# Moving the transposes of a hybrid decoder trunk into longer bursts: both heads of a differential pair in one step, all blocks of rotated queries and keys in one step

## The chip, the core and the metric

The kernel runs on one NeuronCore of a Trainium2 chip. The metric is the device time of one execution in microseconds, as the median of several runs. Beside the runs there is one execution recorded by the hardware profiler, from which all rows below come. Its engines are called PE (TensorE matmuls; its weight loads are PEld), DVE (VectorE), ACT (ScalarE), POOL (GpSimd) and SP (SyncE, which issues the DMAs).

## The reference, cut to what matters

Two layers over a sequence of 256 tokens and 1024 features. Each layer has a mixer of three head groups and a cross attention to a memory of 256 rows; a last RMSNorm follows.

```python
def hybrid_mixer(hn, ...):
    proj = hn @ w_in
    (mq, mk, mv, mg, dq_, dk_, dv_, dg, sq, sk, sv, sg) = jnp.split(proj, cuts, axis=-1)
    a_o = moba_attention(rope(mq), rope(mk), mv)             # 6 heads of 64; here plain causal softmax
    b_o = diff_attention(rope(dq_), rope(dk_), dv_, lam, ...)  # 4 heads, two softmaxes each
    c_o = stick_breaking_attention(sq, sk, sv)               # 6 heads of 64
    merged = concat([a_o * silu(mg), b_o * silu(dg), c_o * silu(sg)])
    return merged @ w_out

def diff_attention(q, k, v, lam, head_norm_g, lam_init):
    p = softmax(causal(q @ k.T * scale))          # sub-heads 2h and 2h+1
    a = p[:, :, 0] - lam * p[:, :, 1]
    o = rms_norm(a @ v, head_norm_g)
    return o * (1.0 - lam_init)

for l in range(2):
    h = h + hybrid_mixer(rms_norm(h), ...)
    h = h + memory_cross_attention(rms_norm(h), rms_norm(mem), ...)
return rms_norm(h)
```

## The kernel before, in words

Every large product is done three times in a reduced fp32 form: the weight tile that a DMA brings (`wraw`) is split by ACT into a rounded part `whi` (line 156) and by DVE into the rest `wlo` (line 157), the activations likewise into `xh` and `xl`, and PE multiplies `whi` with `xh`, `wlo` with `xh` and `whi` with `xl`. `load_next` issues the load and the two splits of one weight tile, five tiles ahead of its use, into six buffers: a split waits until PE has done with the tile that lay in its buffer.

**Order on PE.** PE's instructions stand in the order in which the Python code emits them. The projections are loops (`w_stationary`, lines 409 to 442; `t_stationary`, lines 444 to 459; `mixed`) which call `tick` after each 12 products of 256 columns or 6 of 512. The attention work is written as generators, called jobs: each `yield pe, wait` says how much PE time the step has just taken, in the code's own clock `self.now`, and how long to wait until the next step is due. `tick` (line 115) adds the products' time to the clock and runs the steps that have come due, between two groups of products. So the constants at the top of the file (`COMBINE_NEXT`, `PT_WAIT` and so on) decide behind which group of products a step stands.

**Order on ACT and DVE.** Each of the two engines works through one list. That list is not in the order of emission: the framework's scheduler chooses it from its own estimate of when each operand is ready. A row of the built program tells it; the source doesn't.

**The steps around the change**, in one mixer:

- `transposed` (line 760) transposes the rotated queries and keys by PE against the identity (line 765), four 128x128 blocks into one PSUM bank, and ACT copies the bank (line 767). It runs for the differential heads (`tj`, two banks, copied to `dT`) beside the projection `T3`, and for the MoBA heads (`tj2` with two banks and `tj3` with one, copied to `mT`) beside the memory keys' projection `K`.
- `diff(c)` for c = 0 and 1 handles two differential heads: scores, softmax numerators, a combination of the two softmaxes on DVE (lines 784 to 790), then the transposes of the two results (`p_transposed`, line 591: three transposes and one ACT copy each). The job with c = 1 then multiplies all four heads with their values (`pv`, line 602), squares the outputs, sums the squares on PE (`row_sums`, line 353), takes the inverse root of the sums on DVE and ACT (`inv_root_rows`, lines 360 to 369: the scaled sums are called `dms`, the root `dy`, a temporary `dt`) and scales the gates 3 and 4 with it (line 820).
- `memory_k` (line 503) runs the projection `K`, whose outputs DVE scales into `xq` (line 510) and splits into `xkT` and `xkl`.
- `moba(c)` (line 836) takes scores, numerators (`numerators`, line 575: DVE masks and takes the maximum at line 581, ACT exponentiates at line 586), the scaling (line 847), transposes and `pv`.
- The output projection `out_part` (line 869) takes its eight inputs in the order of `OUT_ORDER`: first the three stick-breaking chunks, then chunks 3 and 4, the differential ones, then the MoBA ones. `more` (line 872) splits each chunk's gate into `xh` on ACT (line 169) and `xl` on DVE (line 170). The inputs from chunks 3 and 4 are `xh3`, `xl3`, `xh4`, `xl4`.

Of the kernel before, what the change touches and what calls it, by code (L numbers as in the profile page):

```python
# [59 lines left out]
DIFF_WAIT, DIFF_PACE, COMBINE_WAIT, COMBINE_NEXT = 6500, 8500, 3750, 1700  # L60
MOBA_WAIT, MOBA_PACE, MOBA_NEXT = 5200, 2000, 1100
X_WAIT, PT_WAIT, ROPE_WAIT = 6000, 950, 8800
# [5 lines left out]
MEM_WAIT, MEM_NORM, X_RSTD = 6000, 28000, 1600  # L68
MOBA_START, SB_START, DIFF_START = 14350, 1500, 1000
PT_LAST = 1300  # L70
MIX_NORM = 14000
ROWS_WAIT, DROWS_WAIT = 11000, 3600
HALVED = 5
# [4 lines left out]
class Trunk:  # L78
# [588 lines left out]
    def mixer(self, l):  # L667
# [15 lines left out]
        def norm():  # L683
            if l == 0:
                squares()
                yield 0, SQ_WAIT
            yield from self.rstd(sq, nr, wait=RSTD_WAIT[l])
            self.tables("silu_and_others")
            yield 0, max(0.0, t2 - self.now)
            gates("W2", o2)  # L690

        njob = self.job(norm(), MIX_NORM if l else FIRST_NORM)
        t2 = self.now + 10500
# [41 lines left out]
        def together(pending, last, first, then):  # L735

            pending.append((first, then))
            if last:
                outs = [f() for f, _ in pending]
                for o, (_, f) in zip(outs, pending):  # L740
                    f(o)
# [16 lines left out]
        jobs = [self.job(sb(c, i > 0), SB_START + SB_PACE * i) for i, c in enumerate((1, 2, 0))]  # L758

        def transposed(x, blocks, dst):  # L760
            for j in range(0, len(blocks), 2):
                ps = self.bank()
                for b in range(2):
                    for t in range(2):
                        nc.tensor.transpose(ps[:, b * 256 + t * 128:b * 256 + t * 128 + 128],  # L765
                                            x[:, t, blocks[j + b] * 128:blocks[j + b] * 128 + 128], self.ident)
                nc.scalar.activation(dst[j // 2], ps, AF.Copy)
                yield 440, 0

        t0 = token("T0", "tq")  # L770
        self.rope(t0, 16, 32, 4, 8)
        dT = [A([128, 512], f"dT{i}") for i in range(2)]
        tj = self.job(transposed(t0, [0, 1, 2, 3], dT), ROPE_WAIT)

        def diff(c):

            self.finish(tj)
            qk = []
            for s in range(4 * c, 4 * c + 4):
                cb, r = s // 4, 32 * (s % 4)  # L780
                qk.append([x[r:r + 32, cb * 256:cb * 256 + 256] for x in dT])
            pr = [self.numerators(ps, 32 ** -0.5) for ps in self.score_quad(qk)]
            yield 1100, DIFF_WAIT
            for j in range(2):
                (p1, r1), (p2, r2) = pr[2 * j:2 * j + 2]
                nc.vector.tensor_scalar(r2, r2, self.lam[:, l:l + 1], None, OP.mult)
                for t, cc in ((0, slice(0, 128)), (1, slice(128, 384))):
                    nc.vector.tensor_scalar(p2[:, cc], p2[:, cc], r2[:, t:t + 1], None, OP.mult)
                    nc.vector.scalar_tensor_tensor(p1[:, cc], p1[:, cc], r1[:, t:t + 1], p2[:, cc],
                                                   OP.mult, OP.subtract)  # L790
            yield 0, COMBINE_WAIT
            pts = []
            for j in range(2):
                pts.append(self.p_transposed(pr[2 * j][0]))
                yield 330, (PT_WAIT if j else COMBINE_NEXT)
            sq = []

            def gated(o):
                q2 = self.work.tile([128, 256], F32, name="sq")
                nc.scalar.activation(q2, o, AF.Square)  # L800
                g = self.gate[3 + len(sq)]
                nc.vector.scalar_tensor_tensor(g, o, self.hg[:, l:l + 1], g, OP.mult, OP.mult)
                sq.append(q2)

            dp.append((pts, c))
            if c == 0:
                return
            outs = [self.pv(lambda j, t: tok["t2"][:, t, 256 + 64 * (2 * c + j):320 + 64 * (2 * c + j)], pts)
                    for pts, c in dp]
            hi, lo = [self.act.tile([128, 512], R, name=n, tag=g) for n, g in (("dnh", "dT0"), ("dnl", "dT1"))]  # L810
            for i, o in enumerate(outs):
                gated(o)
                self.split(sq[i], hi[:, i * 256:i * 256 + 256], lo[:, i * 256:i * 256 + 256])
            yield 1440, DROWS_WAIT
            ps = self.row_sums(self.halfm, hi, lo, 512)
            ms, y, t = [self.work.tile([128, 512], F32, name=n, tag="prob", bufs=5) for n in ("dms", "dy", "dt")]
            self.inv_root_rows(ps, -1.0 / 64, y, t, ms)
            for i in range(2):
                g = self.gate[3 + i]
                nc.vector.tensor_tensor(g, y[:, i * 256:i * 256 + 256], g, OP.mult)  # L820
            yield 480, 0

        tok["t3"] = token("T3", "t3")

        dj = [self.job(diff(c), DIFF_START + DIFF_PACE * c) for c in range(2)]
        t2 = tok["t2"] = token("T2", "t2")
        self.rope(t2[:, :, 0:256], 4, 64, 8, 0)
        t1 = token("T1", "tq")
        self.rope(t1, 8, 64, 8, 0)

        mT = [A([128, 512], f"mT{i}") for i in range(3)]
        tj2 = self.job(transposed(t1, [0, 1, 2, 3], mT[0:2]), ROPE_WAIT)
        tj3 = self.job(transposed(t2, [0, 1], mT[2:3]), ROPE_WAIT)
        blk = lambda i: mT[i // 2][:, (i % 2) * 256:(i % 2) * 256 + 256]

        def moba(c):
# [14 lines left out]
            for j in range(2):  # L851
                pts.append(self.p_transposed(ps[j]))
                yield 330, (PT_LAST if j else MOBA_NEXT)
            together(mp, c > 0, lambda: self.pv(lambda j, t: tok["t3"][:, t, 64 * (2 * c + j):64 * (2 * c + j) + 64],
# [282 lines left out]
```

## Time and profile before

| | before |
|---|---|
| median of 3 runs | 400.91 us (400.55 to 401.03) |
| the profiled execution | 399.81 us, of which its span is 398.1 us |
| PE busy | 390.6 us (98% of the span) |
| DVE busy, ACT busy | 320.8 us (81%), 282.4 us (71%) |
| granted TensorE clock, mean | 0.999 |
| DMA | 64.10 MB, mean 161 GB/s |

The span runs from the first to the last instruction; the profiled execution's own time is 1.71 us longer. Busy time of PE counts overlapping, pipelined matmuls once, and their ends are modelled, so what a matmul costs PE is read from the distance between two starts, not from its duration.

### The profile page before, as it was taken

How to read it: one execution, taken by the hardware profiler on the slowest of the kernel's cores; microseconds unless marked ns; L12 is line 12 of the kernel's file. 1: busy time of each engine (PE TensorE's matmuls, PEld its weight loads, DVE VectorE, ACT ScalarE, POOL GpSimd, SP SyncE). 2: the span in 40 equal slices, each digit the busy share in tenths (PEclk: the TensorE clock that was granted, in tenths of full speed). 3: DMA queues.
4: the chain of work that ended last, by engine and by line, in shares of the span. 5: the costliest groups of instructions: out<-in, count | busy, mean ns of one | idle time of the engine just before them, and what ended most of it. 6: DMA issues, size and time to landing. Idle time of an engine off the chain costs nothing.

```text
span 398.1 us, 7706 instructions
## 1 busy us (share of the span) xinstructions
PE 390.6 (98%) x2803; PEld 355.2 (89%) x2803; DVE 320.8 (81%) x784; ACT 282.4 (71%) x593; POOL 43.7 (11%) x109
## 2 busy tenths in 40 slices
PE   8999999999999999999999999999999999999993
PEld 8999988777899989988999999888788999998983
DVE  5988868788969869889797864876997896797964
ACT  7889588776866868559486934879687667675843
POOL 5688950000000000000000000000000000000000
PEclk9999999999999999999999999999999999999999
DMA  8995794334353343721747765443346433361002
GB/s 287 351 321 173 244 314 151 132 108 138 131 186 130 107 156 109 239 80 53 265 121 267 242 210 169 160 158 105 94 154 225 132 120 127 108 212 53 1 2 105
DMA packets 19190, 64.10 MB, mean 161 GB/s; under 512 B 2384, under 2 KB 2768, under 8 KB 19152
## 3 DMA queue, kind: packets, MB, share of 16 engines
q1 hardware_dynamic: 19152, 63.61, 47.2%
q8 instruction: 22, 0.36, 0.4%
q14 instruction: 16, 0.13, 0.1%
HBM read 62.55 MB, written 1.05 MB: 160 GB/s over the span
## 4 chain that ended last, share of the span: by engine, by line
PE 89%; DVE 6%; ACT 3%; issue 1%; ACTq 0%; DVEq 0%
PE bank L428 39%; PE bank L455 8%; PE bank L457 7%; PE bank L456 7%; PE bank L1013 3%; PE bank L607 2%; PE bank L596 2%; DVE wlo L157 2%; PE bank L948 1%; PE bank L659 1%; ACT whi L156 1%; PE bank L765 1%; PE bank L483 1%; PE bank L482 1%; PE bank L481 1%
## 5 line engine op out<-in xcount | busy, mean ns | idle before, releaser
L157 DVE TENSOR_TENSOR wlo<-wraw,whi 128x1024 fp32r<-128x1024 f32 (+2 forms) x118 | 137.3, 1169 | 33.8 <-ACT whi L156 32.3
L156 ACT ACTIVATE whi<-wraw 128x1024 fp32r<-128x1024 f32 (+2 forms) x118 | 118.2, 1011 | 40.0 <-PE bank L428 19.5
L428 PE MATMUL bank<-xh,whi 128*128 128x256 f32 x416 | 119.1, 287 | 0.0
L428 PE MATMUL bank<-xh,wlo 128*128 128x256 f32 x416 | 117.3, 283 | 0.0
L428 PE MATMUL bank<-xl,whi 128*128 128x256 f32 x416 | 117.1, 283 | 0.0
L428 PEld LDWEIGHTS bank<-xh,whi 128*128 128x128 f32 x416 | 79.4, 191 | 1.4 <-issue 0.7
L428 PEld LDWEIGHTS bank<-xh,wlo 128*128 128x128 f32 x416 | 79.5, 192 | 0.2 <-DVE wlo L157 0.2
L428 PEld LDWEIGHTS bank<-xl,whi 128*128 128x128 f32 x416 | 79.5, 192 | 0.0
L455 PE MATMUL bank<-whi,xh 128*128 128x512 f32 x128 | 52.0, 407 | 0.0
L456 PE MATMUL bank<-wlo,xh 128*128 128x512 f32 x128 | 50.1, 392 | 0.0
L457 PE MATMUL bank<-whi,xl 128*128 128x512 f32 x128 | 50.1, 391 | 0.0
L586 ACT ACTIVATE prob<-prob,mx 128x128 f32<-128x128 f32 (+1 forms) x56 | 24.8, 445 | 10.9 <-DVE mx L583 10.9
L455 PEld LDWEIGHTS bank<-whi,xh 128*128 128x128 f32 x128 | 24.1, 188 | 6.2 <-issue 2.0
L457 PEld LDWEIGHTS bank<-whi,xl 128*128 128x128 f32 x128 | 24.0, 188 | 5.3
L456 PEld LDWEIGHTS bank<-wlo,xh 128*128 128x128 f32 x128 | 24.1, 188 | 4.1
L314 ACT ACTIVATE xh<-h 128x256 fp32r<-128x256 f32 x32 | 14.5, 497 | 6.6 <-DVE h L310 6.3
L428 PE MATMUL bank<-mh,whi 128*128 128x256 f32 x64 | 18.8, 294 | 0.0
L581 DVE CUSTOM_DVE_ANT_0 prob<-bank,cmask 128x128 f32<-128x128 f32 (+1 forms) x56 | 17.9, 350 | 0.3
L428 PE MATMUL bank<-ml,whi 128*128 128x256 f32 x64 | 18.1, 282 | 0.0
L428 PE MATMUL bank<-mh,wlo 128*128 128x256 f32 x64 | 18.1, 282 | 0.0
L325 ACT ACTIVATE sq<-h 128x256 f32<-128x256 f32 x28 | 11.4, 410 | 6.4 <-DVE sqacc L326 5.9
L647 DVE SCALAR_TENSOR_TENSOR sbr<-sbe,sbr 128x384 f32<-128x384 f32 x12 | 6.4, 556 | 11.7 <-ACT sbr L646 11.7
(285 smaller groups left out, 790.2 us busy)
## 6 DMA issues: line engine op xcount, KB each, us to landing
wraw<-in_w_dram SPq DMA_DIRECT2D x107, 512.0 KB, 3.8
wraw<-in_w_dram SPq DMA_DIRECT2D x10, 256.0 KB, 4.4
wraw<-in_memT_dram SPq DMA_DIRECT2D x4, 512.0 KB, 4.6
h<-in_xT_dram SPq DMA_DIRECT2D x3, 256.0 KB, 4.5
out_dram<-wraw SPq DMA_DIRECT2D x2, 288.0 KB, 2.2
wraw<-in_gfin_dram SPq DMA_DIRECT2D x1, 512.0 KB, 4.9
out_dram<-wraw SPq DMA_DIRECT2D x2, 224.0 KB, 2.2
h<-in_xT_dram SPq DMA_DIRECT2D x1, 280.0 KB, 3.0
```

What stands on the lines that cost most here:

```text
L156: nc.scalar.activation(hi[:, c], raw[:, c], AF.Copy)
L157: nc.vector.tensor_tensor(lo[:, c], raw[:, c], hi[:, c].bitcast(F32), OP.subtract)
L314: nc.scalar.activation(h, src[k], AF.Copy, scale=g)
L325: nc.scalar.activation(s, src[k], AF.Square)
L428: nc.tensor.matmul(outs[m], st[:, kk, c], x[k], start=k + p == 0 and m % 2 == 0, stop=k == n - 1 and p == 2, skip_group_check=True)
L455: nc.tensor.matmul(outs[t], xh[k][:, c], whi[:, kk, :], start=first, stop=False)
L456: nc.tensor.matmul(outs[t], xh[k][:, c], wlo[:, kk, :], start=False, stop=False)
L457: nc.tensor.matmul(outs[t], xl[k][:, c], whi[:, kk, :], start=False, stop=last)
L581: nc.vector.tensor_tensor_reduce(s[:, c], ps[:, c], self.cmask[:, c], 1.0, -3.0e38, OP.add, OP.max, accum_out=m[:, t:t + 1])
L586: nc.scalar.activation(s[:, c], s[:, c], AF.Exp, bias=m[:, t:t + 1], scale=scale, accum_out=sm[:, t:t + 1])
L596: nc.tensor.transpose(ps[:, b * 128:b * 128 + 128], p[:, b * 128:b * 128 + 128], self.ident)
L1013: nc.tensor.matmul(out[:, 0:w], x[:, r], w_, start=m == 0 and not seeded, stop=m == 11, skip_group_check=True)
```

## The change

Two generators yield less often. `transposed` now emits all its banks in one step and reports their PE time together. `diff` waits `COMBINE_NEXT` first and then emits the transposes of both heads of its pair in one step, followed by a wait of the new constant `DIFF_PT` (1400) in place of `PT_WAIT` (950). The line numbers of the changed file are one larger from line 71 on and one or two larger behind `transposed`.

```diff
@@ -68,6 +68,7 @@
 PT_LAST = 1300
+DIFF_PT = 1400
 MIX_NORM = 14000
@@ -758,6 +759,7 @@
         def transposed(x, blocks, dst):
+
             for j in range(0, len(blocks), 2):
                 ps = self.bank()
                 for b in range(2):
@@ -765,7 +767,7 @@
                 nc.scalar.activation(dst[j // 2], ps, AF.Copy)
-                yield 440, 0
+            yield 220 * len(blocks), 0
@@ -789,10 +791,9 @@
             yield 0, COMBINE_WAIT
-            pts = []
-            for j in range(2):
-                pts.append(self.p_transposed(pr[2 * j][0]))
-                yield 330, (PT_WAIT if j else COMBINE_NEXT)
+            yield 0, COMBINE_NEXT
+            pts = [self.p_transposed(pr[2 * j][0]) for j in range(2)]
+            yield 660, DIFF_PT
             sq = []
```

No instruction is added or removed on any engine, and the list of DMAs is the same. On PE, per layer, four pairs of bursts become one: 4 and 4 transposes beside `T3`; 3 and 3 beside `T1` (for c = 0); 3 and 3 at the end of `T1` (for c = 1); and beside `K` a burst of 8 and, 12 products later, one of 4 become one burst of 12 at the place of the 8. With the new constants, 24 products of `K` instead of 12 stand between the last transposes of `diff(1)` and its `pv`; from `pv` to the sums of squares there are 36 products in both. So the sums stand one group of 12 products later. What the scheduler made of this on ACT and DVE is shown at three places of layer 0; layer 1 has the same orders.

The first place is DVE's list around the inverse root of the sums of squares (beside `K`), from there on; `wlo` is the split of a weight tile. Before:

```order
L363 TENSOR_SCALAR dms_1738<-bank_1735 128x512
L157 TENSOR_TENSOR wlo_1752<-wraw_1750,whi_1751 128x1024
L366 TENSOR_TENSOR dt_1740<-dy_1739 128x512
L367 TENSOR_TENSOR dt_1740<-dt_1740,dms_1738 128x512
L368 TENSOR_SCALAR dt_1740<-dt_1740 128x512
L369 TENSOR_TENSOR dy_1739<-dy_1739,dt_1740 128x512
L157 TENSOR_TENSOR wlo_1794<-wraw_1792,whi_1793 128x1024
L820 TENSOR_TENSOR gate3_618<-dy_1739,gate3_618 128x256
L820 TENSOR_TENSOR gate4_621<-dy_1739,gate4_621 128x256
L510 TENSOR_TENSOR xq_1828<-bank_1651,rbcm_1174 128x256
L510 TENSOR_TENSOR xq_1832<-bank_1651,rbcm_1174 128x256
L170 TENSOR_TENSOR xl3_2059<-gate3_618,xh3_2058 128x256
```

The same place of the changed kernel:

```order
L158 TENSOR_TENSOR wlo_1737<-wraw_1735,whi_1736 128x1024
L364 TENSOR_SCALAR dms_1756<-bank_1753 128x512
L158 TENSOR_TENSOR wlo_1800<-wraw_1798,whi_1799 128x1024
L367 TENSOR_TENSOR dt_1758<-dy_1757 128x512
L368 TENSOR_TENSOR dt_1758<-dt_1758,dms_1756 128x512
L511 TENSOR_TENSOR xq_1828<-bank_1651,rbcm_1174 128x256
L369 TENSOR_SCALAR dt_1758<-dt_1758 128x512
L511 TENSOR_TENSOR xq_1832<-bank_1651,rbcm_1174 128x256
L370 TENSOR_TENSOR dy_1757<-dy_1757,dt_1758 128x512
L171 TENSOR_TENSOR xkl0_1647<-xq_1828,xkT_1646 128x256
L821 TENSOR_TENSOR gate3_618<-dy_1757,gate3_618 128x256
L821 TENSOR_TENSOR gate4_621<-dy_1757,gate4_621 128x256
```

One weight split moved ahead of `dms`, another stands ahead of the first `dt` instead of behind `dy`, and the split `xl3` is no longer here.

The second place is ACT's list at the same point, the logarithm and the exponential of the inverse root (`dy`). Before:

```order
L156 ACTIVATE whi_1751<-wraw_1750 128x1024
L364 ACTIVATE dy_1739<-dms_1738 128x512
L365 ACTIVATE dy_1739<-dy_1739 128x512
L156 ACTIVATE whi_1793<-wraw_1792 128x1024
L767 ACTIVATE mT0_1643<-bank_1780 128x512
```

And in the changed kernel:

```order
L157 ACTIVATE whi_1736<-wraw_1735 128x1024
L365 ACTIVATE dy_1757<-dms_1756 128x512
L157 ACTIVATE whi_1799<-wraw_1798 128x1024
L366 ACTIVATE dy_1757<-dy_1757 128x512
L769 ACTIVATE mT0_1643<-bank_1780 128x512
```

The second weight split moved between the logarithm and the exponential.

The third place is DVE's list in the MoBA numerators, 53 rows behind the scaling of gate 3, in the changed kernel:

```order
L582 ISA prob_1981,mx_1982<-bank_1965,cmask_127 128x256
L582 ISA mx_1982 128x1
L158 TENSOR_TENSOR wlo_1994<-wraw_1992,whi_1993 128x1024
L584 TENSOR_SCALAR mx_1982<-mx_1982 128x2
L589 RECIPROCAL sum_1975<-sum_1975 128x2
L171 TENSOR_TENSOR xl3_2059<-gate3_618,xh3_2058 128x256
L848 TENSOR_SCALAR prob_1970<-prob_1970,sum_1975 128x128
L848 TENSOR_SCALAR prob_1970<-prob_1970,sum_1975 128x256
L171 TENSOR_TENSOR xl4_2063<-gate4_621,xh4_2062 128x256
```

and, beside it, the first products of PE that use `xl3`, which stand at the same row of PE's list in both kernels (here the kernel before):

```order
L596 MATMUL bank_2046<-ident_119,prob_1901 128x128 x3
L596 MATMUL bank_2052<-ident_119,prob_1924 128x128 x3
L428 MATMUL bank_1856<-xh3_2058,whi_1654 128x256
L428 MATMUL bank_1856<-xh3_2058,wlo_1655 128x256
L428 MATMUL bank_1856<-xl3_2059,whi_1654 128x256
```

The splits `xl3` and `xl4` moved from ahead of all the MoBA numerators to behind all of their maxima, and their user on PE did not move.

## Rows read from the trace of the kernel before

**Rows 1.** The page: busy us (share of the span) and instructions of each engine.

```profile
PE 390.6 (98%) x2803; PEld 355.2 (89%) x2803; DVE 320.8 (81%) x784; ACT 282.4 (71%) x593; POOL 43.7 (11%) x109
```

**Rows 2.** Chain that ended last: shares by engine, and pieces (start, us, what).

```profile
PE 89%; DVE 6%; ACT 3%; issue 1%; ACTq 0%; DVEq 0%
...
146.91 1.64 PE bank L428 x12
...
148.57 1.07 ACT whi L156
...
184.14 2.85 PE bank L948 x20
```

**Rows 3.** Timeline of PE, four transposes beside T3 (start us, us, instruction).

```profile
82.07 0.39 PE L457 MATMUL bank<-whi,xl 128*128 128x512 f32 x1
82.30 0.60 PE L765 MATMUL bank<-ident,tq 128*128 128x128 f32 x4
82.65 0.48 PE L455 MATMUL bank<-whi,xh 128*128 128x512 f32 x1
82.97 0.39 PE L456 MATMUL bank<-wlo,xh 128*128 128x512 f32 x1
```

**Rows 4.** Timeline of PE, six transposes and the first products with xh3, xl3.

```profile
136.81 0.28 PE L428 MATMUL bank<-xl,whi 128*128 128x256 f32 x1
136.93 0.82 PE L596 MATMUL bank<-ident,prob 128*128 128x128 f32 x6
137.50 0.36 PE L428 MATMUL bank<-xh,whi 128*128 128x256 f32 x1
137.71 0.28 PE L428 MATMUL bank<-xh,wlo 128*128 128x256 f32 x1
137.82 0.29 PE L428 MATMUL bank<-xl,whi 128*128 128x256 f32 x1
```

**Rows 5.** Timeline of PE, last transposes of diff(1), its pv, its sums of squares.

```profile
110.03 0.49 PE L596 MATMUL bank<-ident,prob 128*128 128x128 f32 x3
...
111.87 0.65 PE L607 MATMUL bank<-pt,t 128*64 128x256 f32 x4
...
117.74 0.40 PE L357 MATMUL bank<-dnh,halfm 128*128 128x512 f32 x1
```

**Rows 6.** Timeline of DVE from the sums of squares on (in brackets: idle before, releaser).

```profile
118.40 0.69 DVE L363 TENSOR_SCALAR dms<-bank 128x512 f32<-128x512 f32 x1 [1.03 <-PE bank L357]
119.03 1.23 DVE L157 TENSOR_TENSOR wlo<-wraw,whi 128x1024 fp32r<-128x1024 f32 x1
120.46 0.69 DVE L366 TENSOR_TENSOR dt<-dy 128x512 f32<-128x512 f32 x1 [0.20 <-ACT dy L365]
...
122.98 1.22 DVE L157 TENSOR_TENSOR wlo<-wraw,whi 128x1024 fp32r<-128x1024 f32 x1
...
125.45 0.41 DVE L170 TENSOR_TENSOR xl<-gate,xh 128x256 fp32r<-128x256 f32 x1
```

**Rows 7.** Timeline of ACT around the inverse root.

```profile
117.94 1.06 ACT L156 ACTIVATE whi<-wraw 128x1024 fp32r<-128x1024 f32 x1 [1.82 <-PE bank L428]
119.13 0.63 ACT L364 ACTIVATE dy<-dms 128x512 f32<-128x512 f32 x1
119.80 0.63 ACT L365 ACTIVATE dy<-dy 128x512 f32<-128x512 f32 x1
121.28 1.06 ACT L156 ACTIVATE whi<-wraw 128x1024 fp32r<-128x1024 f32 x1 [0.85 <-PE bank L428]
```

**Rows 8.** Busy us (instructions) of PE, PEld, DVE, ACT, POOL; clock; one stretch per layer.

```profile
120.46:137.45 16.99, 16.99 (x147) 16.40 (x146) 16.07 (x62) 11.61 (x33) 0.00 (x0) 1.00 0.37 125
313.10:330.10 17.00, 17.00 (x147) 16.41 (x146) 16.08 (x62) 11.61 (x33) 0.00 (x0) 1.00 0.38 124
```

**Rows 9.** The same view, late cross attention of layer 1: 28 transposes in 36 PE operations.

```profile
374.10:378.10 4.00, 4.00 (x39) 4.00 (x38) 3.62 (x12) 4.00 (x11) 0.00 (x0) 1.00 0.00 0
```

**Rows 10.** Timeline of PE: the 15 warm-up products at the start.

```profile
1.24 3.54 PE L1064 MATMUL bank<-warm 128*128 128x256 f32 x15 [1.24 <-DVE warm L1041]
```

## The prediction

> **What bounds the kernel now.** I read the busy times first, then the chain of waits, then the timelines of PE, DVE and ACT around the bursts. PE is busy for 390.6 of the 398.1 us of the span [rows 1], and the chain that ended last lies on PE for 89% of it [rows 2]: nearly every product starts as soon as the one ahead of it lets it, so a microsecond that PE waits anywhere is a microsecond on the end. Only from 148.57 to 184.14 us does the chain run over ACT and DVE, and it enters there through a weight split that follows a PE product at once [rows 2]; what delays PE ahead of it delays that stretch too. So two questions decide. Does a longer burst cost PE less? And does anything that PE reads come later than PE gets to it?
>
> **The bursts themselves.** The reader should look at starts, since matmuls overlap. Beside T3 the last product ahead of four transposes starts at 82.07 and the second one behind them at 82.97 [rows 3]. These 0.90 us hold two products of 512 columns, which without a burst start 0.23 us apart (82.07 to 82.30), and four transposes: 0.90 - 0.46 = 0.44 us, 0.11 each. For six transposes the same reading gives 137.71 - 136.81 = 0.90 us, less two products of 256 columns at 0.12 (136.81 to 136.93): 0.66 us, again 0.11 each [rows 4]. A burst of four and one of six cost the same per transpose, so there is no price per burst that merging could save. What rounding leaves open is about 0.01 us a burst. Four bursts fewer per layer, eight in all, are worth 0 to 0.08 us; I take 0.04 us off. This is all that the change can save on PE, since no instruction goes away.
>
> **What moves behind the bursts.** The second dT burst comes earlier, its copy on ACT too, and the users of dT (the scores) don't move: nothing waits there. The first of each pair of differential transposes comes later, but its user, `pv` of diff(1), moves too: it now follows the last transposes by 24 products instead of 12. The 12 products more take 12 x 0.12 = 1.44 us [rows 4], against 1.84 us from the last transposes to `pv` before [rows 5], so the ACT copies have more room, not less. All mT copies are there at the latest when they were. These edits I cost at nothing; what covers them is PE's own products in between, and if that cover were gone, one copy of about half a microsecond would show.
>
> But the sums of squares stand 36 products behind `pv` in both kernels, so they come 1.44 us later: at 117.74 + 1.44 = 119.18 instead of 117.74 [rows 5]. And there DVE's and ACT's lists have changed. I follow them for layer 0, all times on the clock of the trace of before.
>
> 1. On DVE a weight split `wlo` now stands ahead of `dms`. Its `whi` is made by ACT from 117.94, after ACT has idled 1.82 us for a PE product to free the buffer, so it can't be made earlier [rows 7]. `wlo` then starts at 119.03 and takes 1.14 us of DVE to the next start (its 1.22 us, less the overlap seen between 122.98 and 124.12) [rows 6]: `dms` starts at 120.2, not at 118.40.
> 2. ACT's logarithm follows 0.73 us after the start of `dms` (118.40 to 119.13), so at 120.9, and takes 0.67 us to the next start [rows 6, 7]. Now the second weight split stands here, at 121.6. Before, ACT waited until 121.28 for its buffer [rows 7], so it need not wait longer. It ends at 121.6 + 1.06 = 122.7, and the exponential behind it at about 123.2.
> 3. DVE has the matching `wlo` ahead of `dt`: 122.7 + 1.14 = 123.9. So `dt` starts at **123.9** instead of 120.46 [rows 6], 3.4 us later: 1.44 from the change's timing, 2.0 from the two weight splits.
> 4. From `dt` on DVE has no room. In the stretch from the start of `dt` to the end of the last scaling of a maximum, 120.46 to 137.45, DVE is busy 16.07 of 16.99 us, in layer 1 16.08 of 17.00 [rows 8]. In the changed list exactly the same work stands between `dt` and `xl3`, but for the two splits `xl3` and `xl4`, 0.41 us each [rows 6]: the same three `wlo`, the same six maxima, the same four scaled heads. That is 16.07 - 0.82 = 15.25 us. Then `xl3` itself takes 0.41. Without a single idle moment, `xl3` is ready at 123.9 + 15.25 + 0.41 = **139.56**. In the kernel before the same split started at 125.45 [rows 6], twelve microseconds ahead of its user.
> 5. PE reads `xl3` at 137.82 [rows 4], and the built order puts its user at the same row of PE's list as before, with the same products and transposes ahead of it. So PE stands still for 139.56 - 137.82 = **1.75 us** (to the nearest 0.05), with the whole output projection behind the waiting product.
>
> What is late next: `xl4` follows two scalings behind `xl3`, at about 140.4, and its first user stands one group of 12 products and six transposes behind that of `xl3`, 12 x 0.12 + 0.66 = 2.1 us, so at about 141.7; it waits for nothing. The later MoBA transposes and `pv` get up to 1.75 us more room. So one wait per layer. Layer 1 has the same orders and the same load [rows 8], so the sum is 2 x 1.75 - 0.04 = 3.46, +3.5 us.
>
> **The bounds of the wait.** If `dt` moved by the 1.44 us alone, to 121.9, `xl3` would be ready at 121.9 + 15.66 = 137.6 and PE would not wait: 0. If both weight splits waited for their buffers again as long as ACT's longest wait here, 1.82 us [rows 7], `dt` would start at 125.7 and PE would wait 3.6 us a layer. I take 1.75, since both buffers are free by rows 7 when the lists reach them; the two ends serve the range and the rivals.
>
> The sum is made against the profiled execution: 399.81 + 3.5 = 403.3 us. That execution lies 1.1 us under the median of the runs, 400.91, so the median after is 400.91 + 3.5 = **404.4 us**, slower by 0.9%. About 0.2%, 0.8 us, is what a measurement of this kernel can tell from no change.
>
> **Rivals.**
>
> *DVE catches up, and nothing changes.* The place is `dt`: if it starts before 137.82 - 15.66 = 122.2 us, `xl3` is in time and only the 0.04 us of the bursts is left: 400.9 us, not slower. For it speaks that the change itself moves the sums by 1.44 us alone, and that 122.2 is 0.3 us beyond that. Against it: both weight splits stand ahead in the lists, and ACT's idle time of 1.82 and 0.85 us ahead of the same splits before [rows 7] shows that PE frees their buffers no earlier. Chance 0.13, of it 0.10 within 0.2% and 0.03 faster, should merged bursts free something that I don't see.
>
> *Half of it is taken back.* In layer 0 the cross attention's chain runs over ACT and DVE from 148.57 to 184.14 [rows 2]. If that stretch started on DVE's own time and not on PE's, PE's wait ahead of it would vanish in a later one: only layer 1 pays, 400.91 + 1.75 = 402.7 us. Against it: the stretch begins with a weight split right behind the PE products of 146.91 [rows 2]. Chance 0.07.
>
> *The clock falls.* A burst of 12 transposes, or a PE that stands for 1.75 us, lets the granted clock drop to its lower level once per layer. A price is in the warm-up: 15 products took 3.54 us there [rows 10] at the lower of the two levels (1.2 GHz), against 15 x 0.12 = 1.80 us at the upper (2.4 GHz) [rows 4], so 1.74 us a fall. On top of the wait that makes 404.4 + 2 x 1.7 = 407.8 us. Against it: 4.0 us of cross attention in layer 1 with 28 transposes in 36 operations kept a granted clock of 1.00 [rows 9]. Chance 0.04.
> The Trainium skill, page "TensorE: Matmul & The Clock Gate", section "Part 4: PE-mode transpose", says that the full clock doesn't engage for transposes, since they don't count as a busy TensorE in the same way; by that rule the longer bursts would bring this third rival's 407.8 us. The trace doesn't bear it out, by the same 1.00.
>
> **How the numbers follow.** The wait on `xl3` in both layers has a chance of 0.76, the rivals 0.13, 0.07 and 0.04. Slower by over 0.2% are the forecast, the second and the third rival: 0.87. Within 0.2%: 0.10, faster: 0.03. For the forecast I allow 0.3 us more or less for `dt` in each layer and as much for the stretch, and the spread of the medians, about 403.4 to 405.3; the range reaches down to the second rival, 402.6, and up to 405.3, and leaves out the first and the third.
>
> **What would show it.** In the trace after: PE idle time ahead of a product of the output projection (line 429) of about 1.75 us, released by DVE's `xl` (line 171), once near 138 and once near 332 us; `dt` (line 367) at about 123.9; DVE without idle time from there to `xl`; PE busy time unchanged, and transposes at 0.11 us in bursts of 8 and 12. Wrong would be a PE without that wait, a wait at another line (a `pt` copy, a maximum), or a burst of 8 that takes clearly less than 0.88 us.

## The result, and the profile after

| | before | after |
|---|---|---|
| median | 400.7 us (400.37 to 401.03, 6 runs) | 403.68 us (403.21 to 404.03, 6 runs) |
| ratio | | 1.0074, 95% interval 1.0061 to 1.0087 |
| the profiled execution | 399.81 us, span 398.1 us | 403.61 us, span 401.5 us |

The change makes the kernel slower by 0.74%, 2.98 us. Of the 3.8 us between the two profiled executions 0.84 us lie in the first 9 us. The change has no part in them: it was the profiled execution of before that started well. Its 200th PE operation starts at 27.26 us, those of the eleven other traces at 27.91 to 28.60.

The page of after: busy us (share of the span) and instructions of each engine, and the chain that ended last by engine.

```profile
PE 391.7 (98%) x2803; PEld 356.3 (89%) x2803; DVE 319.8 (80%) x784; ACT 282.1 (70%) x593; POOL 45.0 (11%) x109
...
PE 77%; DVE 15%; ACT 4%; issue 2%; DMA 1%; SPq 0%; ACTq 0%; DVEq 0%
```

Every engine has the instructions it had, and its busy time is within 1.3 us of what it was [rows 1]; the chain, however, now goes over DVE for 15% instead of 6% [rows 2]. Something that DVE makes has become late. The list of PE's waits of after says which (instruction, releaser: us in total, times, the longest):

```profile
PE bank L429 <- DVE xl L171: 2.1, 2, 1.1
```

This line is new: two waits of 1.1 us ahead of a product of the output projection, released by DVE's `xl`. The list has two more, 1.2 us at the start of the program, which before had too [rows 10], and one of 0.2 us for a weight split 7 us into it. The timeline of PE of after at the place of [rows 4], and the same place in layer 1 (start us, us, instruction, in brackets idle before and releaser):

```profile
138.42 0.28 PE L429 MATMUL bank<-xh,wlo 128*128 128x256 f32 x1
139.76 0.39 PE L429 MATMUL bank<-xl,whi 128*128 128x256 f32 x1 [1.06 <-DVE xl L171]
139.98 0.28 PE L429 MATMUL bank<-xh,whi 128*128 128x256 f32 x1
...
333.79 0.39 PE L429 MATMUL bank<-xl,whi 128*128 128x256 f32 x1 [1.06 <-DVE xl L171]
```

Read by starts: the product at 138.42 would have been followed by the next at 138.54, 0.12 later; it came at 139.76. PE stood for 1.22 us (the profile's 1.06 counts from the end of the product ahead). The product behind the wait takes 0.22 instead of 0.12 to the next start, so 1.32 us in all. Layer 1 has the same wait.

Why `xl` came late is on DVE and ACT, where PE's place is 0.72 us later than in the trace of before (138.54 against 137.82 [rows 4]). DVE of after:

```profile
119.74 1.23 DVE L158 TENSOR_TENSOR wlo<-wraw,whi 128x1024 fp32r<-128x1024 f32 x1 [1.80 <-ACT whi L157]
120.89 0.69 DVE L364 TENSOR_SCALAR dms<-bank 128x512 f32<-128x512 f32 x1
123.22 1.23 DVE L158 TENSOR_TENSOR wlo<-wraw,whi 128x1024 fp32r<-128x1024 f32 x1 [1.65 <-ACT whi L157]
124.36 0.69 DVE L367 TENSOR_TENSOR dt<-dy 128x512 f32<-128x512 f32 x1
125.08 0.69 DVE L368 TENSOR_TENSOR dt<-dt,dms 128x512 f32<-128x512 f32 x1
125.69 0.42 DVE L511 TENSOR_TENSOR xq<-bank,rbcm 128x256 f32<-128x256 f32 x1
126.02 0.42 DVE L369 TENSOR_SCALAR dt<-dt 128x512 f32<-128x512 f32 x1
126.36 0.42 DVE L511 TENSOR_TENSOR xq<-bank,rbcm 128x256 f32<-128x256 f32 x1
126.69 0.68 DVE L370 TENSOR_TENSOR dy<-dy,dt 128x512 f32<-128x512 f32 x1
127.29 0.42 DVE L171 TENSOR_TENSOR xkl<-xq,xkT 128x256 fp32r<-128x256 f32 x1
127.62 0.76 DVE L821 TENSOR_TENSOR gate<-dy,gate 128x256 f32<-128x256 f32 x2
128.29 0.42 DVE L171 TENSOR_TENSOR xkl<-xq,xkT 128x256 fp32r<-128x256 f32 x1
...
139.30 0.40 DVE L171 TENSOR_TENSOR xl<-gate,xh 128x256 fp32r<-128x256 f32 x1
```

and ACT of after, around the inverse root:

```profile
121.61 0.63 ACT L365 ACTIVATE dy<-dms 128x512 f32<-128x512 f32 x1 [1.90 <-DVE dms L364]
122.14 1.04 ACT L157 ACTIVATE whi<-wraw 128x1024 fp32r<-128x1024 f32 x1
123.09 0.62 ACT L366 ACTIVATE dy<-dy 128x512 f32<-128x512 f32 x1
```

Against [rows 6] and [rows 7]: a weight split stands ahead of `dms` (119.74), and a second one between the logarithm (121.61) and the exponential (123.09) on ACT and so ahead of `dt` on DVE (123.22). `dt` starts at 124.36. Behind it DVE does not stop until `xl`, as this view shows (busy us of PE, PEld, DVE, ACT, POOL; granted clock, DMA share, GB/s):

```profile
124.36:139.30 14.94, 14.34 (x122) 13.54 (x120) 14.90 (x61) 11.57 (x34) 0.00 (x0) 1.00 0.32 107
```

DVE is busy for 14.90 of the 14.94 us; it is PE that now stands still in this stretch, from 138.70 on. The granted clock is 1.00 there, as in the 12 transposes that now come in a row (PE's timeline around them, and the same view of their stretch):

```profile
121.66 0.28 PE L429 MATMUL bank<-ml,whi 128*128 128x256 f32 x1
121.78 1.04 PE L767 MATMUL bank<-ident,tq 128*128 128x128 f32 x8
122.66 0.60 PE L767 MATMUL bank<-ident,t 128*128 128x128 f32 x4
123.02 0.36 PE L429 MATMUL bank<-mh,whi 128*128 128x256 f32 x1
123.22 0.28 PE L429 MATMUL bank<-mh,wlo 128*128 128x256 f32 x1
```

```profile
121.70:123.00 1.30, 1.30 (x15) 1.30 (x14) 0.00 (x0) 1.30 (x2) 0.00 (x0) 1.00 0.78 224
```

From 121.66 to 123.22 there are two products at 0.12 and twelve transposes: 1.56 - 0.24 = 1.32 us, 0.11 each, as in bursts of four and six [rows 3, 4].

### The profile page after: what moved, and what is told of

The parts are those of the page before. It is cut to its first block, busy times and chain, and to the rows that moved or that the text cites. A ratio compares the mean times of both kernels' runs of the same rounds, so it can differ in the third digit from the quotient of the medians.

```text
span 401.5 us, 7711 instructions
## 1 busy us (share of the span) xinstructions
PE 391.7 (98%) x2803; PEld 356.3 (89%) x2803; DVE 319.8 (80%) x784; ACT 282.1 (70%) x593; POOL 45.0 (11%) x109
## 4 chain that ended last, share of the span: by engine, by line
PE 77%; DVE 15%; ACT 4%; issue 2%; DMA 1%; SPq 0%; ACTq 0%; DVEq 0%
PE bank L429 31%; PE bank L456 8%; PE bank L457 7%; PE bank L458 7%; DVE wlo L158 4%; PE bank L1014 3%; ACT whi L157 2%; PE bank L608 2%; DVE prob L582 2%; PE bank L949 1%; PE bank L660 1%; PE bank L597 1%; DMA wraw<-in_w_dram 1%; PE bank L477 1%; PE bank L483 1%
```

## The experiments

All were timed in five rounds against the kernel before, whose median lay between 401.02 and 401.19 us in these comparisons. Edits are against the changed kernel, unless said. For the first four runs my theory was the late split: only the place of the one split `xl` in DVE's list is wrong. Its rivals were the bursts themselves, which could hold PE or ACT up, and the load of DVE: with later sums DVE has no slack, wherever the split stands. The fourth run decided for the load of DVE, and from then on my theory is this: the bursts cost nothing; the later value products bring later sums, later sums bring a late `dt`, and DVE has no slack behind it. A rival is left for it too: the later value products delay something else. The times expected for the first four start from the 400.7 us of before in the section on the result; beside these runs it took 0.3 us more.

### Only the rotated blocks merged

```diff
-            yield 0, COMBINE_NEXT
-            pts = [self.p_transposed(pr[2 * j][0]) for j in range(2)]
-            yield 660, DIFF_PT
+            pts = []
+            for j in range(2):
+                pts.append(self.p_transposed(pr[2 * j][0]))
+                yield 330, (PT_WAIT if j else COMBINE_NEXT)
```

> Only the rotated queries and keys are transposed in one step; the differential heads keep their two steps. In the built order the sums of squares stay at their old place on PE, and xl3 and xl4 stay ahead of the MoBA numerators on DVE. The late split (the theory): no wait of PE for xl, time 400.6 us or 0.0 to 0.2 under the kernel before. The burst itself (rival 1: a longer lump of transposes and copies makes the others late): a part of the 3 us shows, 401.5 us or more. The load of DVE (rival 2: the 1.44 us by which the sums come later are enough, wherever the split stands in the list): 400.6 us, since the sums are not later here.

Measured: 401.14 us, ratio 1.0002 (0.9993 to 1.0011); no wait for `xl`. By the time, the longer bursts of rotated blocks neither help nor hurt.

### Both merges, with the old wait of 950

```diff
-DIFF_PT = 1400
+DIFF_PT = 950
```

> The whole change, but with the new constant DIFF_PT at 950 in place of 1400: all bursts are merged, pv of diff(1) and the sums stand one group of 12 products earlier, and the built order has xl3 ahead of the numerators again. The late split: no wait of PE for xl, 400.3 to 400.7 us. The burst itself: 403.7 us as the change. The load of DVE: 400.5 us.

Measured: 400.88 us, ratio 0.9996 (0.9988 to 1.0005). PE's only wait by the profile is the one at the start. The whole change without its new constant can't be told from before.

### No merge, only the new wait (edit of the kernel before)

```diff
-                yield 330, (PT_WAIT if j else COMBINE_NEXT)
+                yield 330, (1400 if j else COMBINE_NEXT)
```

> The kernel before with nothing but the wait behind the last differential transposes raised from 950 to 1400: no burst is merged, but pv and the sums stand one group of 12 products later and xl3 stands behind the numerators as in the change. The late split: PE waits some 1.2 us per layer at the product with xl3, 403.3 to 403.9 us. The burst itself: 400.7 us, no wait. The load of DVE: 403.5 us.

Measured: 404.1 us, ratio 1.0077 (1.0064 to 1.0091), and PE's waits are those of after:

```profile
PE bank L428 <- DVE xl L170: 2.1, 2, 1.1
```

The constant alone makes the loss: its 450 ns more on the code's clock push the value products, and with them the sums, behind the next group of 12 products.

### The split of chunks 3 and 4 put early in DVE's list

```diff
-        more(OUT_ORDER[3:5])
+        with self.urgent():
+            more(OUT_ORDER[3:5])
```

> The change as it is, PE order unchanged, but the splits of chunks 3 and 4 are given to the scheduler as urgent, so that xl3 and xl4 stand 3 rows behind the scaling of gate 3 on DVE, ahead of all MoBA numerators; the sums still come 12 products later than in the kernel before. The late split: no wait of PE for xl, 400.3 to 400.8 us. The burst itself: 403.7 us. The load of DVE: the wait stays or moves to the MoBA transposes (their numerators now stand behind the two splits), 402.5 us or more.

Measured: 404.03 us, ratio 1.0074 (1.0061 to 1.0086). This was a miss of mine: I had held the place of the split for the whole matter. `xl` is now made at 128.86 and nobody waits for it, but PE waits about as long elsewhere:

```profile
PE bank L597 <- DVE prob L848: 2.2, 2, 1.1
```

```profile
139.97 0.49 PE L597 MATMUL bank<-ident,prob 128*128 128x128 f32 x3
141.56 0.70 PE L597 MATMUL bank<-ident,prob 128*128 128x128 f32 x3 [1.11 <-DVE prob L848]
```

Six such transposes without a stop take 0.57 us to the next start (136.93 to 137.50 [rows 4]), so the second three would have stood some 0.29 us behind the first; they came 1.59 behind, 1.3 us late. Taking work out of the list ahead of one user puts it ahead of the next one. So it is not one split that is late but everything that DVE does here.

### The sums back at their place, the rest of the change kept

```diff
-ROWS_WAIT, DROWS_WAIT = 11000, 3600
+ROWS_WAIT, DROWS_WAIT = 11000, 2150
```

> The changed kernel with DROWS_WAIT at 2150 instead of 3600: the merged bursts stay, and the value products still start 12 products late, but the two sums over the squares stand where they stood before the change (12 products of 0.12 us earlier than in the changed kernel), and with them dms, log, exp and dt. Theory 'late sums' (what is late is only the start of the chain sums, dms, log, exp, dt on a DVE without slack): dt about 3 us earlier, no wait of PE ahead of the xl products, 400.5 to 401.2, ratio 0.999 to 1.001. Rival 'late value products' (the merged transposes and the value products at their later place hold DVE and ACT up by themselves): 403.7, ratio 1.007, wait of 1.1 us per layer still there.

Measured: 401.07 us, ratio 1.0004 (0.9995 to 1.0013), no wait for `xl`. The later transposes and value products are harmless by themselves; the loss hangs on the later sums.

### The low parts of the memory keys on POOL

```diff
-            self.split(k, *self.xk[m])
+            hi, lo = self.xk[m]
+            self.nc.scalar.activation(hi, k, AF.Copy)
+            self.nc.gpsimd.tensor_tensor(lo, k, hi.bitcast(F32), OP.subtract)
```

> The changed kernel with the four low parts of the split memory keys (xkl) computed on POOL instead of DVE; the late sums stay. They take DVE 4 x 0.335 = 1.34 us between dt and the late split xl. Theory 'DVE's list' (DVE has no slack from dt on, and all of its work up to 139.3 us is late by the same 1.2 us): the wait of 1.22 us per layer goes or leaves under 0.2 us, 400.5 to 401.3. Rival 'chain' (the wait is set by the dependent steps from the sums to xl or to the probabilities, not by the amount of DVE work): 403.3 to 404.1, with the wait at xl or at the second three transposes. Rival 'POOL beside DVE is slow': DVE's instructions beside POOL's get longer than their 0.34 us, and part of the wait stays, 401.5 to 403.

Measured: 402.41 us, ratio 1.0038 (1.0026 to 1.0051): the third theory's range. The timelines of POOL and of DVE show the price:

```profile
127.01 0.74 POOL L514 TENSOR_TENSOR xkl<-xq,xkT 128x256 fp32r<-128x256 f32 x1 [72.07 <-ACT xkT L513]
128.27 0.73 POOL L514 TENSOR_TENSOR xkl<-xq,xkT 128x256 fp32r<-128x256 f32 x1 [0.52 <-ACT xkT L513]
129.17 0.74 POOL L514 TENSOR_TENSOR xkl<-xq,xkT 128x256 fp32r<-128x256 f32 x1 [0.17 <-ACT xkT L513]
131.05 1.20 POOL L514 TENSOR_TENSOR xkl<-xq,xkT 128x256 fp32r<-128x256 f32 x1 [1.15 <-ACT xkT L513]
```

```profile
127.06 1.24 DVE L370 TENSOR_TENSOR dy<-dy,dt 128x512 f32<-128x512 f32 x1
128.22 0.41 DVE L511 TENSOR_TENSOR xq<-bank,rbcm 128x256 f32<-128x256 f32 x1
128.56 1.63 DVE L823 TENSOR_TENSOR gate<-dy,gate 128x256 f32<-128x256 f32 x2
130.11 0.41 DVE L511 TENSOR_TENSOR xq<-bank,rbcm 128x256 f32<-128x256 f32 x1
```

`dy` takes 1.24 us where it took 0.68 in after, the two gates 1.63 where they took 0.76. From start to next start that is 1.16 + 1.55 = 2.71 us (127.06 to 128.22, 128.56 to 130.11), against 0.60 + 0.67 = 1.27 in after (126.69 to 127.29, 127.62 to 128.29): 1.44 us lost against 1.34 saved. No wait for `xl` is left; in its place a group of MoBA value products comes late, by 0.94 us in layer 0 and 0.73 in layer 1. That the time still fell by some 1.3 us against after I ascribe in part to the order of DVE's list, which the framework chose anew; no run tests that. Another 0.4 us of it lie outside the span (1.68 to 1.73 us in these runs, 2.08 to 2.14 in those of after).

### The sums another 12 products later

```diff
-ROWS_WAIT, DROWS_WAIT = 11000, 3600
+ROWS_WAIT, DROWS_WAIT = 11000, 5000
```

> The changed kernel with DROWS_WAIT at 5000 instead of 3600: the two sums stand another 12 products (1.43 us) later. On ACT the weight split that stood between log and exp now stands ahead of log, and a copy of the rotated queries between log and exp. Theory 'DVE's list, set by dt': dms at about 122.3, log after the first copy at about 123.3, exp at about 124.2, dt at about 125.0, which is 0.6 us later than in the changed kernel: the wait grows from 1.22 to 1.6 to 2.0 us per layer, 404.3 to 405.3. Rival 'each product that the sums come later is paid in full': wait 1.22 + 1.43 = 2.65 per layer, 406.3 to 407. Rival 'the two weight splits are what is late': nothing grows, 403.5 to 404.

Measured: 404.2 us, ratio 1.0079 (1.0065 to 1.0092).

```profile
138.86 0.28 PE L429 MATMUL bank<-xh,wlo 128*128 128x256 f32 x1
140.48 0.39 PE L429 MATMUL bank<-xl,whi 128*128 128x256 f32 x1 [1.34 <-DVE xl L171]
```

```profile
123.05 1.23 DVE L158 TENSOR_TENSOR wlo<-wraw,whi 128x1024 fp32r<-128x1024 f32 x1
125.06 0.69 DVE L367 TENSOR_TENSOR dt<-dy 128x512 f32<-128x512 f32 x1 [0.79 <-ACT dy L366]
```

The wait is 140.48 - 138.98 = 1.50 us, 0.28 more than in after, though the sums are 1.43 later. I had 1.6 to 2.0 and a median 0.1 above what came: the first theory by its kind, its size too large. The reason is on ACT and DVE: the weight split that stood behind the logarithm is now made ahead of it, so `dt` stands only 13.92 us ahead of PE's product (138.98 - 125.06) against 14.18 in after (138.54 - 124.36), 0.26 less. The wait follows `dt`, not the sums.

### The logarithm straight from the sums' bank

For this inverse root alone (`direct`); `self.eps` is a new tile that holds EPS:

```diff
-        nc.vector.tensor_scalar(ms, src, mul, EPS, OP.mult, OP.add)
-        nc.scalar.activation(y, ms, AF.Ln)
+        if direct:
+            nc.scalar.activation(y, src, AF.Ln, scale=mul, bias=self.eps)
+            nc.vector.tensor_scalar(ms, src, mul, EPS, OP.mult, OP.add)
+        else:
+            nc.vector.tensor_scalar(ms, src, mul, EPS, OP.mult, OP.add)
+            nc.scalar.activation(y, ms, AF.Ln)
...
-            self.inv_root_rows(ps, -1.0 / 64, y, t, ms)
+            self.inv_root_rows(ps, -1.0 / 64, y, t, ms, True)
```

> The changed kernel with the sums at their late place, but ACT takes the logarithm straight from the sums' bank (scale and bias in the instruction), so log does not wait for dms; in ACT's order log and exp then stand together, ahead of the weight split that stood between them, and on DVE dt stands ahead of the second weight split. The sums stay 12 products late. Theory 'DVE's list, set by dt': log at about 120.7, exp at 121.3, dt at about 122, some 2.4 us earlier than in the changed kernel and under 1.7 us later than before the change: no wait, 400.5 to 401.2. Rival 'late sums alone' (1.44 us later cannot be made up, whatever stands behind them): a wait of 0.3 to 1 us per layer remains, 401.5 to 403.

Measured: 400.82 us, ratio 0.9992 (0.9983 to 1.0001), no wait for `xl`. ACT's list:

```profile
120.64 0.69 ACT L367 ACTIVATE dy<-bank,epsc 128x512 f32<-128x512 f32 x1 [0.84 <-PE bank L360]
121.36 0.64 ACT L372 ACTIVATE dy<-dy 128x512 f32<-128x512 f32 x1
122.07 1.06 ACT L157 ACTIVATE whi<-wraw 128x1024 fp32r<-128x1024 f32 x1
```

```profile
119.82 1.23 DVE L158 TENSOR_TENSOR wlo<-wraw,whi 128x1024 fp32r<-128x1024 f32 x1 [1.80 <-ACT whi L157]
...
122.02 0.69 DVE L373 TENSOR_TENSOR dt<-dy 128x512 f32<-128x512 f32 x1
...
123.36 1.22 DVE L158 TENSOR_TENSOR wlo<-wraw,whi 128x1024 fp32r<-128x1024 f32 x1
```

The sums are as late as in after, and the first weight split still stands ahead of them; only the second one has gone from between the logarithm and the exponential, and stands behind `dt` on DVE (123.36). `dt` starts at 122.02, and PE reaches the product at 138.62: 16.60 us ahead, and that is enough, though only just. The framework made `xl` early here too (127.02), as in the experiment with the early split, so the two can be compared: DVE scales the last MoBA maximum 0.47 us after PE reaches the product, there 1.77 us after it, with a wait of 1.3 us. So late sums need not cost anything; the loss also needs what stands between the sums and `dt` in the changed kernel, the second weight split and the way over `dms`. Which of these two counts for more the run doesn't tell, since it takes both away. And because it does without the way over `dms`, `dt` is only 0.76 us later against PE than in before, not 1.44: what the later sums alone would cost no run shows.

### The low parts of the memory keys later on DVE

The four instructions are kept on DVE in a fixed place. The first version puts them behind the splits of the next sublayer's input:

```diff
+        kq = [self.act.tile([128, 512], F32, name=f"kq{i}", tag=f"dT{i}") for i in range(2)]
+        self.kq = [kq[m // 2][:, m % 2 * 256:m % 2 * 256 + 256] for m in range(4)]
...
-            k = self.work.tile([128, 256], F32, name="xq")
-            self.nc.vector.tensor_tensor(k, outs[m], self.mr["bc"], OP.mult)
-            self.split(k, *self.xk[m])
+            self.nc.vector.tensor_tensor(self.kq[m], outs[m], self.mr["bc"], OP.mult)
+            self.nc.scalar.activation(self.xk[m][0], self.kq[m], AF.Copy)
...
         out_part(1, range(5, 8), 6)
+        for k, (hi, lo) in zip(self.kq, self.xk):
+            self.tc.keep_in_program_order(nc.vector.tensor_tensor(lo, k, hi.bitcast(F32), OP.subtract))
```

> The changed kernel with the four low parts of the split memory keys (xkl, 4 x 0.335 = 1.34 us of DVE) still on DVE, but at a fixed place behind the splits of the next sublayer's input (near 155 us and 348 us, some 19 us ahead of the first product that reads them) instead of between dt and the late split xl; their products wait in the two tiles that held the halves of the squares. Sums, log, exp and dt stay as late as in the changed kernel; POOL does nothing. Theory 'DVE's list' (all that DVE does between dt and 139.3 us is one list without slack, and the wait is what it is too long): 1.34 us less in the list against a wait of 1.22 us, so no wait over 0.2 us per layer, neither at the products of xl nor at the transposes of the probabilities, 400.4 to 401.4. Rival 'chain' (the dependent steps behind the late sums set the wait, not the amount of DVE's work): 403.3 to 404.1. Rival 'only moved': the next sublayer's input splits or what follows them are 1.34 us late instead, and PE waits there, 401.5 to 403.5.

Measured: 405.09 us, ratio 1.0112 (1.009 to 1.0135), slower than after. No wait for `xl` or the MoBA probabilities is left, but these are new, and one of 0.5 us in the cross attention beside them:

```profile
PE bank L936 <- ACT pth L170: 1.5, 1, 1.5
PE bank L358 <- DVE nl L171: 1.5, 2, 0.7
```

```profile
159.81 1.43 DVE L891 TENSOR_TENSOR xkl<-kq,xkT 128x256 fp32r<-128x256 f32 x4
```

The four instructions came at 159.81, 5 us later than I had meant, ahead of the sums of squares of the next sublayer, where DVE has no gap either. That is the third theory, and above its range. The second version moves them up by two calls of `out_part`, to a gap of 1.37 us that DVE had near 149 us:

```diff
         more(OUT_ORDER[5:])
+        for k, (hi, lo) in zip(self.kq, self.xk):
+            self.tc.keep_in_program_order(nc.vector.tensor_tensor(lo, k, hi.bitcast(F32), OP.subtract))
```

> As e9_k_splits_later, but the four low parts of the memory keys stand on DVE directly behind the last split of the merged heads (xl of head group 7), near 149 us and 344 us, where DVE waited 1.37 us for a weight tile. Sums, log, exp and dt stay as late as in the changed kernel. Theory 'DVE's list, paid where it has no gap': no wait at the products of xl, at the transposes of the probabilities, nor behind them in the next sublayer, 400.4 to 401.4, ratio 0.999 to 1.001. Rival 'chain': what e9 cost behind 160 us hid nothing of the first wait, and a wait of 1 us per layer near 138 and 333 us stays, 403 to 404. Rival 'the next sublayer is late anyway': no wait near 138 us, but the two row sums of the next sublayer wait again by some 0.9 us per layer, 402 to 403.5.

Measured: 401.2 us, ratio 1.0006 (0.9996 to 1.0016). PE's only wait is the one at the start.

```profile
124.24 0.68 DVE L367 TENSOR_TENSOR dt<-dy 128x512 f32<-128x512 f32 x1
...
148.81 1.42 DVE L889 TENSOR_TENSOR xkl<-kq,xkT 128x256 fp32r<-128x256 f32 x4
```

`dt` starts at 124.24 and PE reaches the product at 138.42: 14.18 us ahead, to the hundredth as in after, where PE waited. With 1.34 us less on DVE in between it doesn't. The framework also moved `xl` forward here, but that alone did nothing in the experiment with the early split.

## Why the prediction was right, and where its size was off

The lead of `dt` over PE's product puts the runs in one row. From the start of `dt` DVE needs 14.94 us to `xl`, 0.40 for it, and PE starts 0.06 later (139.70 to 139.76): 15.40 us.

| kernel | `dt` starts ahead of PE's product by | 15.40 less this | wait in layer 0 |
|---|---|---|---|
| before | 137.82 - 120.46 = 17.36 us | below 0 | 0 |
| sums at the old place | 139.04 - 121.67 = 17.37 | below 0 | 0 |
| logarithm from the bank | 138.62 - 122.02 = 16.60 | below 0 | 0 |
| after | 138.54 - 124.36 = 14.18 | 1.22 | 1.22 |
| sums later still | 138.98 - 125.06 = 13.92 | 1.48 | 1.50 |
| memory keys in the gap | 138.42 - 124.24 = 14.18 | 1.22 - 1.34, below 0 | 0 |

Only the row of after gave the 15.40. The row with the sums later still tests it in size; the other four test it only by the absence of a wait, since in all of them `xl` stands further ahead in DVE's list. Nor is that list the same in each: with the sums at the old place and with the logarithm from the bank one more weight split, 1.14 us, stands in it behind `dt`, so their leads have to reach about 16.5 us, which the second one does by less than 0.1.

For step 4 below, the steps of the root in before, behind the `dt` of [rows 6]:

```profile
121.19 0.69 DVE L367 TENSOR_TENSOR dt<-dt,dms 128x512 f32<-128x512 f32 x1
121.91 0.43 DVE L368 TENSOR_SCALAR dt<-dt 128x512 f32<-128x512 f32 x1
122.37 0.69 DVE L369 TENSOR_TENSOR dy<-dy,dt 128x512 f32<-128x512 f32 x1
```

- **The bursts: right that they are worth next to nothing, but not that they have no price.** It is 0.11 us per transpose in bursts of 4, 6 and 12, and both merges alone are within 0.1% of before. But by the starts, PE's lag behind the trace of before fell where bursts were merged: by 0.13 us in layer 0 and 0.12 in layer 1, 0.03 to 0.06 for each pair beside products of 512 columns and nothing for the pair beside `K`. I had 0.04 us for both layers together, and 0.08 at most. The traces with both merges and the old wait and with the memory keys in the gap give 0.13 in layer 0 and 0.08 to 0.12 in layer 1. My reading of two single bursts, rounded to hundredths, was too coarse for it; 0.25 us in all is still nothing that the times can tell.
- **Steps 1 and 2, the lists of DVE and ACT: right.** On the clock of before (0.72 earlier) `dms` came at 120.17 (said 120.2), the logarithm at 120.89 (120.9), the split behind it at 121.42 (121.6). The logarithm holds ACT for 0.53 us to the next start, where I took 0.67: before, the exponential behind it had to wait for its result.
- **Step 3, `dt`: 123.64 instead of 123.9**, by that 0.14 and by rounding up on the way. That the 1.44 us of the sums alone would bring no wait was in the bounds of the wait; no run shows it. With the logarithm from the bank `dt` is late by 0.76 us only, and PE does not wait.
- **Step 4 was mis-sized: 14.94 us from `dt` to `xl` instead of 15.25.** I took DVE's busy time as a sum that does not depend on the order. It does: a DVE operation that needs the result of the one ahead starts 0.72 us behind it (`dt` 121.19 to 121.91 in before), an independent one 0.61 behind the same 0.69 us (125.08 to 125.69 in after). The changed list puts a scaling of the memory keys behind two steps of the root, and so hides 0.1 us twice: 0.61 and 0.34 us to the next start instead of 0.72 and 0.46. I also took the two `xl` out of the list with 0.41 us each, though in before each held it for 0.34 to the next start (125.45 to 125.79), which alone would have made the sum 0.15 longer. Against that sum the list of after is 0.46 us shorter: the two steps of the root are about half of it, and the rest is spread over small operations that had idle time behind them in before and are followed at once in after.
- **Step 5, the wait:** 123.64 + 14.94 + 0.40 + 0.06 - 137.82 = 1.22 us instead of 1.75, once per layer at the line, the releaser and the place that were named. "Late next: nothing" held in after. It did not hold as a rule: as soon as the split is put early, the MoBA transposes are late by 1.3 us.
- **The sum: 2.98 us (2.4 to 3.5 by the interval) instead of 3.5, and part of that is luck.** From 9 us to the end, PE's lag behind the trace of before grows by 2.57 us: 2 x 1.33 for the two waits, less 0.13 and 0.12 for the bursts, and 0.16 more in small delays between the layers. Another 0.4 us is outside the span: the six runs of after spend 2.08 to 2.14 us there, the 70 of before that were timed beside the experiments 1.66 to 1.76. The two make up the 2.98. Nothing in the prediction stands for the 0.4; it makes up for part of the wait that I had too long. Which part of the change brings it stays open: with both merges and the old wait it is 1.76 to 1.83 us, with the new wait alone 1.70 to 1.75, with the memory keys in the gap 2.04 to 2.12.
- **Rivals.** "DVE catches up" would have needed `dt` before 122.2 on the clock of before; it is what happens in the run with the logarithm from the bank. "Half of it is taken back" was not seen: PE's lag behind before was 2.04 us behind the wait of layer 0 and 2.08 ahead of that of layer 1. "The clock falls" was not seen: the granted clock was 1.00, its upper level, in the twelve transposes and around the wait. So the Trainium skill's sentence on the full clock and transposes (page "TensorE: Matmul & The Clock Gate", section "Part 4: PE-mode transpose") did not carry over to bursts of this length. The price that I put on a fall of the clock rests on the distance of the warm-up products alone, 0.24 against 0.12 us: the profile's view of that stretch gives a granted clock of 1.00, so no row shows the lower level itself.

None of the versions is faster than before beyond what can be told from no change. In the best of them PE waits nowhere but at the start, so no wait is left to take away.

## What to carry to other kernels

Merging small bursts on a full PE is worth what a switch costs, and the rows with the bursts tell its order of size before any edit: here at most 0.06 us for two bursts made one. What a retimed step costs is decided on the engine that serves it later: find the last instruction that starts its run without slack (here `dt`), add up that engine's list to PE's user, and compare the lead with the list; a delay inside the slack is free, and beyond it the delay of that instruction is paid in full (0.26 us later, 0.28 more waiting), at whichever user comes first. If such a list is too long, moving an operation helps only into a gap that the timeline shows, and not onto an engine that slows the first one down.

## What was not expected of the hardware

- **POOL and DVE hold each other up.** Beside a POOL subtraction of 0.74 us, started 0.05 us earlier, DVE's `dy` took 1.24 us instead of 0.68; beside two more, two gates took 1.63 instead of 0.76. A fourth POOL subtraction, at 131.05, started 0.61 us behind a weight split of DVE and took 1.20 us itself, while that split took 1.21, as it does alone. But DVE's `xq` at 128.22, with one operand in a PSUM bank, took 0.41 beside POOL's of 128.27, no more than alone. The Trainium skill, page "SBUF — State Buffer", section "Who interferes with whom", says this: a DVE instruction with two SBUF inputs contends with a GpSimd instruction that reads SBUF, since they share a port pair under an exclusive lock, and one with at most one SBUF input, outside the two-port modes, does not. The rows agree on both halves.
- **The order of independent work on DVE is worth 0.1 us per dependent step that it separates**, as in step 4: with the same instructions, two steps of the root took 0.61 and 0.34 us to the next start instead of 0.72 and 0.46.
